# TensorE issues in the order of tracing in four phases of a two-block transformer kernel

## The chip, the cores and the metric

One core of one Trainium2 chip. A core has TensorE (PE, matmuls and transposes, results into PSUM banks), VectorE (DVE), ScalarE (ACT), GpSimd (POOL) and SyncE (SP, which issues the loads). The metric is the device time of one execution in microseconds, and lower is better.

## The reference

Two transformer blocks on one sequence of 512 tokens and 1024 features, in float32. The first block has four mixers (convolution, sparse attention, latent attention, stick breaking) and a feed forward. The second has a gated linear recurrence beside a windowed attention, an attention into 256 memory tokens, and a gated feed forward with a convolution. Cut to the lines that the change touches:

```python
x = x + jnp.square(jax.nn.relu(h2 @ ffn_w1[l])) @ ffn_w2[l]            # first feed forward
...
proj = n @ w_in                                                        # second block's mixers
...
y_rec = o.astype(n.dtype) @ w_br_rec                                   # o: the gated recurrence
qa = partial_rotary(q_a.reshape(B, S, ATT_Q_HEADS, ATT_HEAD_DIM), positions)
ka = partial_rotary(k_a.reshape(B, S, ATT_KV_HEADS, ATT_HEAD_DIM), positions)
y_att = window_gqa_sink(qa, ka, va, sink) @ w_br_att                   # 8 heads, window of 128
merged = jax.nn.sigmoid(gate_r) * y_rec + jax.nn.sigmoid(gate_a) * y_att
return merged @ w_out
...
s = jnp.einsum('bshd,bmhd->bhsm', q, k).astype(jnp.float32) * (MEM_HEAD_DIM ** -0.5)   # memory attention
p = jax.nn.softmax(s, axis=-1).astype(v.dtype)
o = jnp.einsum('bhsm,bmhd->bshd', p, v).reshape(B, S, D_MODEL)
return o @ w_o
...
return (jax.nn.silu(gc) * u) @ w_down                                  # second feed forward
```

## The kernel before, in words

**Data.** The activations stay in SBUF, transposed, as eight tiles x0 to x7 of 128 features by 512 tokens. A matrix product is done in three matmuls, of the high and low parts of both operands (`mm3`, L183 to L185): hi by hi, lo by hi, hi by lo. Weights come from HBM through `wraw`; ACT rounds them to `whi` (L258), and DVE takes the difference as `wlo` (L259). `whi` and `wlo` have two buffers each.

**Phases**, with their place in the profiled execution: the first block's mixers (0 to about 309 us, not touched by the change), the first feed forward `ffn1` (to about 697), the second block's mixers `mixers2` (to about 1047), the memory attention `memory` (to about 1245), the second feed forward `ffn2` (to the end).

**What sets the order.** The program is traced once, call by call. Each instruction then goes to its engine's own list; the framework's scheduler, which models the engines, orders each list, and may let a later traced instruction overtake one that would wait. An engine runs its list strictly in that order, and waits at an instruction whose inputs or whose buffer are not ready. Beside that, the code writes an order by hand: `pipeline` runs the units of an attention in three stages (logits, transposes of the probabilities, product with V), and between the stages calls `fill`, which draws triples of matmuls from a generator `side()` of independent work.

**mixers2.** The recurrence ends with `gla_out`, whose `tr` transposes (L1634) give the operand recT (`rT0` to `rT3`). Then comes the windowed attention. `window` rotates q and k in place (DVE, L1649 to L1652), and then traces its preparation without a `fill` in between:

```python
for c in range(4):
    qT += self.trans_pair(wp, [qkv[:, t, c * P:(c + 1) * P] for t in range(NT)], eighth, f"wq{c}")
...
    kd = self.T(wp, [P, NT, 2, 64], F32, "wkd", 1)
...
    kT.append(self.trans_hl(wp, [kd[:, t].rearrange("p a d -> p (a d)") for t in range(NT)], P, None, f"wk{kh}", ps="pT"))
```

Each `trans_pair` makes four transposes of q into one PSUM bank `pT` (L866), and then `split_pair` reads that bank four times in turn: ACT `wq h` (L880), DVE (L881), ACT `wq l`, DVE. `trans_hl` does the same for k from `wkd`, a copy that POOL makes (L1667), with one read by ACT (`wk h`, L191) and one by DVE (`wk l`, L192). There is one `pT` bank, and one `wkd`. The 32 units of the attention (4 token tiles by 8 heads) follow, with L889 and L890 as their logits, and `self.pipeline(units, 0.6, (0, 2, 3))` draws from `side()`: recT by w_br_rec, and then the gates, columns 4352 on of w_in. Behind the units stands `trans_hl` four times on the attention's result `oN` (16 transposes, L854), in the same `pT` bank.

**memory.** `token_bcast` (L431 on) turns the norm's row sums into a tile by two diagonal matrices in `nsq` (DVE, L437) and a matmul `pt` (L439). The buffers of `nsq` are shared with the squares that POOL adds into `nacc` (L417). A head's probabilities times V are twelve matmuls into a bank `o` (one buffer), which ACT and DVE read out as H2h, H2l, H3h, H3l (L191, L192).

Of the kernel before, what the change touches and what calls it, by code (L numbers as in the profile page):

```python
# [148 lines left out]
class Kern:  # L149
# [382 lines left out]
    def run(self):  # L532
        nc, tc, A = self.nc, self.tc, self.A
        self.setup()
        self.x = [self.T(self.xp, [P, S], F32, f"x{k}") for k in range(8)]
        self.mixers1()
        if self.upto in ("sb", "nsa", "mla", "conv", "x1"):
            return
        self.ffn1()
        if self.upto == "x2":  # L540
            return
        self.mixers2()
        if self.upto in ("gla", "win"):
            return
        self.memory()
        if self.upto in ("x3", "x4"):
            return
        self.ffn2()


    def mixers1(self):
# [1390 lines left out]
```

## Time and profile before

| | |
|---|---|
| time of the kernel before, median of 3 runs | 1624.3 us (1623.17 to 1624.51) |
| profiled execution, its own time | 1626.29 us |
| profiled execution, span from the first to the last instruction | 1624.6 us |
| mean granted clock of TensorE | 0.995 of full |
| TensorE busy | 1591.5 us, 98% |
| TensorE weight loads | 1341.8 us, 83% |
| DVE, ACT, POOL busy | 921.0, 667.0, 174.9 us |

The profiled execution took 2.0 us longer than the median, and 1.7 us more than its span. TensorE is busy nearly throughout: all its idle time together is 1624.6 - 1591.5 = 33.1 us. Matmuls are pipelined, so their durations overlap, and the time that one takes of the engine is read from start to start.

### The profile page before, as it was taken

The page shows a single profiled execution, that of the slowest core. Times are in us where ns is not written, and L with a number is a line of the kernel's source. Part 1 is how long each engine was busy: PE and PEld are TensorE (multiplying, and loading weights), DVE is VectorE, ACT ScalarE, POOL GpSimd, SP SyncE. Part 2 cuts the span into 40 slices and gives each one's busy share as a digit, 9 for nine tenths or more (in the row PEclk, how much of TensorE's full clock was granted, in tenths as well). Part 3 has the DMA queues.
Part 4 walks back from the last instruction along what each step waited for, and adds up shares of the span by engine and source line. Part 5 has one row for each costly group of instructions (what it writes and reads, how often), then busy time and mean ns, then how long its engine had stood idle before and what let it go on. Part 6 is the DMA issues. An engine that isn't in the chain of part 4 may idle for free.

```text
span 1624.6 us, 20813 instructions
## 1 busy us (share of the span) xinstructions
PE 1591.5 (98%) x8049; PEld 1341.8 (83%) x8049; DVE 921.0 (57%) x1503; ACT 667.0 (41%) x1172; POOL 174.9 (11%) x185
## 2 busy tenths in 40 slices
PE   8999999999999999999999999999999999999998
PEld 6798888788888888878888788888988888888886
DVE  6666885644223434475766565664667556526662
ACT  5675554544123423334333354353544233222332
POOL 0121110200000001121110000330002111001110
PEclk9999999999999999999999999999999999999999
DMA  7242131232322223221222211323332333232331
GB/s 225 67 126 85 33 117 40 66 102 92 101 94 98 97 94 100 88 89 55 73 72 78 65 40 59 115 96 118 126 98 84 99 98 97 94 101 91 101 120 52
DMA packets 108118, 148.15 MB, mean 91 GB/s; under 512 B 7887, under 2 KB 58868, under 8 KB 108020
## 3 DMA queue, kind: packets, MB, share of 16 engines
q1 hardware_dynamic: 107876, 146.72, 28.3%
q8 instruction: 63, 1.03, 0.3%
q14 instruction: 35, 0.29, 0.1%
q10 hardware_dynamic: 144, 0.11, 0.0%
HBM read 142.31 MB, written 4.20 MB: 90 GB/s over the span
## 4 chain that ended last, share of the span: by engine, by line
PE 90%; DVE 4%; ACT 2%; issue 1%; POOL 1%; DMA 1%; SPq 0%; POOLq 0%; DVEq 0%; ACTq 0%
PE mm L183 25%; PE mm L185 25%; PE mm L184 25%; PE o L844 2%; PE lv L1570 2%; PE pT L833 1%; PE o L1613 1%; DVE wlo L259 1%; ACT whi L258 1%; PE L L889 1%; DMA wraw<-w_in_dram 1%; DMA wraw<-w_down_dram 1%; PE o L183 0%; PE o L185 0%; PE L L890 0%
## 5 line engine op out<-in xcount | busy, mean ns | idle before, releaser
L259 DVE TENSOR_TENSOR wlo<-wraw,whi 128x1024 fp32r<-128x1024 f32 (+4 forms) x268 | 319.5, 1194 | 439.2 <-ACT whi L258 434.5
L258 ACT ACTIVATE whi<-wraw 128x1024 fp32r<-128x1024 f32 (+4 forms) x268 | 270.4, 1010 | 536.9 <-PE mm L184 470.2
L417 POOL TENSOR_TENSOR nacc<-nacc,nsq 128x512 f32<-128x512 f32 x24 | 37.3, 1553 | 508.7 <-ACT nsq L415 507.6
L1866 POOL TENSOR_TENSOR fz<-fz,fu 128x512 f32<-128x512 f32 x22 | 37.4, 1698 | 269.6 <-ACT fz L1865 269.6
L461 DVE TENSOR_TENSOR x<-mm,x 128x512 f32<-128x512 f32 x72 | 48.9, 687 | 19.1 <-PE mm L185 18.8
L183 PE MATMUL mm<-H4h,whi 128*128 128x512 f32 x147 | 59.3, 404 | 0.0
L183 PE MATMUL mm<-H0h,whi 128*128 128x512 f32 x139 | 55.8, 402 | 2.9 <-ACT whi L258 2.9
L183 PE MATMUL mm<-H6h,whi 128*128 128x512 f32 x147 | 58.1, 399 | 0.4 <-ACT H6h L194 0.4
L183 PE MATMUL mm<-H7h,whi 128*128 128x512 f32 x147 | 58.3, 397 | 0.0
L185 PE MATMUL mm<-H4h,wlo 128*128 128x512 f32 x147 | 57.6, 392 | 0.7 <-DVE wlo L259 0.7
L183 PE MATMUL mm<-H5h,whi 128*128 128x512 f32 x147 | 58.1, 395 | 0.0
L185 PE MATMUL mm<-H6h,wlo 128*128 128x512 f32 x147 | 57.7, 393 | 0.0
L185 PE MATMUL mm<-H5h,wlo 128*128 128x512 f32 x147 | 57.7, 393 | 0.0
L184 PE MATMUL mm<-H6l,whi 128*128 128x512 f32 x147 | 57.7, 393 | 0.0
L184 PE MATMUL mm<-H5l,whi 128*128 128x512 f32 x147 | 57.4, 391 | 0.0
L184 PE MATMUL mm<-H4l,whi 128*128 128x512 f32 x147 | 57.4, 391 | 0.0
L185 PE MATMUL mm<-H7h,wlo 128*128 128x512 f32 x147 | 57.4, 390 | 0.0
L184 PE MATMUL mm<-H7l,whi 128*128 128x512 f32 x147 | 57.3, 390 | 0.0
L185 PE MATMUL mm<-H2h,wlo 128*128 128x512 f32 x139 | 54.5, 392 | 1.1 <-DVE wlo L259 1.1
L183 PE MATMUL mm<-H3h,whi 128*128 128x512 f32 x139 | 55.4, 399 | 0.0
L183 PE MATMUL mm<-H2h,whi 128*128 128x512 f32 x139 | 55.2, 397 | 0.0
L183 PE MATMUL mm<-H1h,whi 128*128 128x512 f32 x139 | 54.9, 395 | 0.0
(1264 smaller groups left out, 4340.1 us busy)
## 6 DMA issues: line engine op xcount, KB each, us to landing
wraw<-ffn_w_dram SPq DMA_DIRECT2D x64, 512.0 KB, 3.6
wraw<-w_up_dram SPq DMA_DIRECT2D x88, 256.0 KB, 2.8
wraw<-w_in_dram SPq DMA_DIRECT2D x36, 512.0 KB, 3.4
wraw<-w_down_dram SPq DMA_DIRECT2D x22, 512.0 KB, 3.6
wraw<-w_mem_kv_dram SPq DMA_DIRECT2D x16, 512.0 KB, 3.7
wraw<-w_in_dram SPq DMA_DIRECT2D x52, 128.0 KB, 2.3
wraw<-w_in_dram SPq DMA_DIRECT2D x20, 256.0 KB, 2.8
wraw<-cmp_w_dram SPq DMA_DIRECT2D x8, 512.0 KB, 4.0
```

The costliest lines, as they stand in the source:

```text
L183: mm(out, a.hi, b.hi, start=start, stop=False, skip_group_check=skip)
L184: mm(out, a.hi, b.lo, start=False, stop=False, skip_group_check=skip)
L185: mm(out, a.lo, b.hi, start=False, stop=stop, skip_group_check=skip)
L258: nc.scalar.activation(hi, raw, AF.Copy)
L259: nc.vector.tensor_sub(lo, raw, hi.bitcast(F32))
L417: eng.tensor_add(nm.acc, nm.acc, sq[:, :nm.N])
L461: self.nc.vector.tensor_add(self.x[k], b, self.x[k])
L833: nc.tensor.transpose(b[:, t * P:(t + 1) * P], st["p"][:, t * P:(t + 1) * P], self.ident)
L844: nc.tensor.matmul(o(), st["pT"][:, t * P:(t + 1) * P], v(t), start=(t == 0), stop=(t == nt - 1))
L889: self.nc.tensor.matmul(out, q[h][:, qs], k.hi[:, ks], start=True, stop=False)
L1570: nc.tensor.matmul(b[:, t * P:(t + 1) * P], ym[:, t * P:(t + 1) * P], mix(X, c, t * P, P), start=True, stop=True)
L1866: nc.gpsimd.tensor_mul(z, z, us[c])
```

## The change

Four phases are traced under a manual schedule for TensorE: there TensorE's list is the order of tracing. The lists of the other engines are still made by the scheduler, which now models a TensorE that doesn't reorder. No instruction is added, taken away or altered.

```diff
--- before
+++ after
@@ -536,16 +536,20 @@
-        self.ffn1()
+        with tc.manual_schedule(engines={mybir.EngineType.PE}):
+            self.ffn1()
...
-        self.mixers2()
+        with tc.manual_schedule(engines={mybir.EngineType.PE}):
+            self.mixers2()
...
-        self.memory()
+        with tc.manual_schedule(engines={mybir.EngineType.PE}):
+            self.memory()
...
-        self.ffn2()
+        with tc.manual_schedule(engines={mybir.EngineType.PE}):
+            self.ffn2()
```

In all, 509 of TensorE's 7547 instructions change their place in its list (none in ffn2), 70 of ACT's 1025 and 121 of DVE's 1503; none of POOL's or SP's. Lines of the changed kernel from L541 on are four higher than the same lines before (L854 is L858, L866 is L870, L889 is L893, L1634 is L1638). Numbers behind a name count tiles as they are made and run 5 to 8 higher after the change; "x4" stands for four such rows.

**First place: TensorE, the preparation of the window attention in mixers2.** Before, from the last transposes `tr` of the recurrence on (recT by w_br_rec into `mm_7857`, `mm_7858`, and q's transposes into the bank `pT_7774`):

```order
L1634 MATMUL tr_7715<-cmat_78,go_7676 128x128 x4
L183 MATMUL mm_7857<-rT0h_6626,whi_7862 128x512
L184 MATMUL mm_7857<-rT0l_6627,whi_7862 128x512
L185 MATMUL mm_7857<-rT0h_6626,wlo_7863 128x512
L183 MATMUL mm_7857<-rT1h_7061,whi_7862 128x512
L184 MATMUL mm_7857<-rT1l_7062,whi_7862 128x512
L185 MATMUL mm_7857<-rT1h_7061,wlo_7863 128x512
L183 MATMUL mm_7858<-rT0h_6626,whi_7862 128x512
L184 MATMUL mm_7858<-rT0l_6627,whi_7862 128x512
L185 MATMUL mm_7858<-rT0h_6626,wlo_7863 128x512
L183 MATMUL mm_7858<-rT1h_7061,whi_7862 128x512
L866 MATMUL pT_7774<-cmat_78,qkv_5936 128x128
```

In the changed kernel, from the same transposes on:

```order
L1638 MATMUL tr_7720<-cmat_78,go_7681 128x128 x4
L870 MATMUL pT_7779<-cmat_78,qkv_5941 128x128 x4
L870 MATMUL pT_7790<-cmat_78,qkv_5941 128x128 x4
L870 MATMUL pT_7801<-cmat_78,qkv_5941 128x128 x4
L870 MATMUL pT_7812<-cmat_78,qkv_5941 128x128 x4
L858 MATMUL pT_7826<-cmat_78,wkd_7823 128x128 x4
L858 MATMUL pT_7838<-cmat_78,wkd_7835 128x128 x4
L893 MATMUL L_7848<-wk0h_7831,wq0h_7784 128x256
L894 MATMUL L_7848<-wk0l_7832,wq0h_7784 128x256
L893 MATMUL L_7856<-wk0h_7831,wq0l_7787 128x256
L894 MATMUL L_7856<-wk0l_7832,wq0l_7787 128x256
L183 MATMUL mm_7862<-rT0h_6631,whi_7867 128x512
```

All 24 transposes and the first four logits now stand directly behind `tr`. The 106 matmuls that stood between them before (recT by w_br_rec, and the first of the gates) come behind, in triples between the stages of the attention's units.

**Second place: TensorE, the transposes of the attention's result `oN` in mixers2.** Before (`mm_8601` and `mm_8602` are gates):

```order
L854 MATMUL pT_8624<-cmat_78,oN_7842 128x128 x4
L183 MATMUL mm_8601<-H1h_5475,whi_8565 128x512
L184 MATMUL mm_8601<-H1l_5476,whi_8565 128x512
L185 MATMUL mm_8601<-H1h_5475,wlo_8566 128x512
L183 MATMUL mm_8602<-H0h_5463,whi_8565 128x512
L184 MATMUL mm_8602<-H0l_5464,whi_8565 128x512
L185 MATMUL mm_8602<-H0h_5463,wlo_8566 128x512
L183 MATMUL mm_8602<-H1h_5475,whi_8565 128x512
L854 MATMUL pT_8633<-cmat_78,oN_7842 128x128 x4
L184 MATMUL mm_8602<-H1l_5476,whi_8565 128x512
```

and likewise for the third and fourth group. In the changed kernel:

```order
L858 MATMUL pT_8629<-cmat_78,oN_7847 128x128 x4
L858 MATMUL pT_8638<-cmat_78,oN_7847 128x128 x4
L858 MATMUL pT_8647<-cmat_78,oN_7847 128x128 x4
L858 MATMUL pT_8656<-cmat_78,oN_7847 128x128 x4
L183 MATMUL mm_8606<-H1h_5477,whi_8570 128x512
L184 MATMUL mm_8606<-H1l_5478,whi_8570 128x512
L185 MATMUL mm_8606<-H1h_5477,wlo_8571 128x512
```

The four groups of transposes stand in a row; the 21 matmuls that stood between them (seven each time) come behind.

**Third place: TensorE, the norm's matmul `pt` in memory.** Before, it stands behind the rest of the matmuls `mm_9172` and `mm_9173` of the mixers' output and five matmuls of the memory's keys (`mm_9370`):

```order
L184 MATMUL mm_9173<-H7l_8944,whi_9265 128x512
L185 MATMUL mm_9173<-H7h_8943,wlo_9266 128x512
L183 MATMUL mm_9370<-mH0h_9035,whi_9302 128x256
L184 MATMUL mm_9370<-mH0l_9036,whi_9302 128x256
L185 MATMUL mm_9370<-mH0h_9035,wlo_9303 128x256
L183 MATMUL mm_9370<-mH1h_9061,whi_9302 128x256
L184 MATMUL mm_9370<-mH1l_9062,whi_9302 128x256
L439 MATMUL pt_9338<-nsq_9335,ones_79 128x256
L185 MATMUL mm_9370<-mH1h_9061,wlo_9303 128x256
```

In the changed kernel (`mm_9179` and `mm_9180` are `mm_9171` and `mm_9172` of before):

```order
L183 MATMUL mm_9179<-H7h_8948,whi_9273 128x512
L184 MATMUL mm_9179<-H7l_8949,whi_9273 128x512
L185 MATMUL mm_9179<-H7h_8948,wlo_9274 128x512
L439 MATMUL pt_9346<-nsq_9343,ones_79 128x256
L183 MATMUL mm_9180<-H6h_8936,whi_9273 128x512
L184 MATMUL mm_9180<-H6l_8937,whi_9273 128x512
```

It moved 17 instructions forward: twelve of the mixers' output and five of the keys now stand behind it.

## Rows read from the trace of the kernel before

**Rows 1.** The page: busy time, share of the span and instructions of each engine.

```profile
PE 1591.5 (98%) x8049; PEld 1341.8 (83%) x8049; DVE 921.0 (57%) x1503; ACT 667.0 (41%) x1172; POOL 174.9 (11%) x185
```

**Rows 2.** Busy time by stretch; columns: length, PE, PEld, DVE, ACT, POOL, clock, DMA.

```profile
697.00:913.00 216.00, 211.23 (x1172) 183.21 (x1171) 145.41 (x224) 83.25 (x136) 27.97 (x20) 0.99 0.23 71
913.00:942.00 29.00, 28.69 (x136) 22.31 (x137) 22.50 (x42) 12.35 (x18) 3.31 (x7) 1.00 0.25 78
942.00:1001.00 59.00, 58.88 (x400) 52.68 (x399) 36.48 (x105) 34.69 (x95) 0.00 (x0) 1.00 0.11 35
...
1245.00:1600.00 355.00, 354.60 (x1572) 292.98 (x1571) 197.42 (x232) 104.10 (x124) 44.82 (x27) 1.00 0.30 95
```

**Rows 3.** Timeline, PE at 911: start, duration, engine, line, operation.

```profile
911.24 0.39 PE L184 MATMUL mm<-H7l,whi 128*128 128x512 f32 x1
911.47 0.39 PE L185 MATMUL mm<-H7h,wlo 128*128 128x512 f32 x1
```

**Rows 4.** Timeline of the window's preparation, from PE, ACT, DVE and POOL.

```profile
918.49 0.32 DVE L1652 TENSOR_TENSOR qkv<-qkv,wu 128x160 f32<-128x160 f32 x1
...
929.53 0.63 PE L866 MATMUL pT<-cmat,qkv 128*128 128x128 f32 x4
...
930.20 0.69 ACT L880 ACTIVATE wq2h<-pT,w 64x512 fp32r<-64x512 f32 x1 [2.14 <-PE pT L866]
...
930.92 0.74 DVE L881 SCALAR_TENSOR_TENSOR wq2h<-pT,w,wq2h 64x512 fp32r<-64x512 f32 x1 [1.53 <-ACT wq2h L880]
...
931.69 0.68 ACT L880 ACTIVATE wq2l<-pT,w 64x512 fp32r<-64x512 f32 x1 [0.81 <-DVE wq2h L881]
...
932.41 0.76 DVE L881 SCALAR_TENSOR_TENSOR wq2l<-pT,w,wq2l 64x512 fp32r<-64x512 f32 x1 [0.75 <-ACT wq2l L880]
...
933.31 0.63 PE L866 MATMUL pT<-cmat,qkv 128*128 128x128 f32 x4
...
939.25 0.60 ACT L191 ACTIVATE wk0h<-pT 128x512 fp32r<-128x512 f32 x1 [0.29 <-PE pT L854]
...
939.35 1.48 POOL L1667 COPY wkd<-qkv 128x256 f32<-128x256 f32 x2 [19.73 <-PE pT L854]
...
940.13 0.68 DVE L192 TENSOR_TENSOR wk0l<-pT,wk0h 128x512 fp32r<-128x512 f32 x1
```

**Rows 5.** Timeline, transposes of `oN` at 1005 (PEld is the weight load).

```profile
1005.62 0.61 PE L854 MATMUL pT<-cmat,oN 128*128 128x128 f32 x4
...
1007.65 0.42 PEld L854 LDWEIGHTS pT<-cmat,oN 128*128 128x128 f32 x4 [0.22 <-DVE rT2l L192]
1007.71 0.60 PE L854 MATMUL pT<-cmat,oN 128*128 128x128 f32 x4
```

**Rows 6.** Timeline around `pt` in memory, from PE, POOL and DVE.

```profile
1086.83 0.39 PE L183 MATMUL mm<-H6h,whi 128*128 128x512 f32 x1
...
1088.41 3.02 POOL L417 TENSOR_TENSOR nacc<-nacc,nsq 128x512 f32<-128x512 f32 x2 [6.05 <-ACT nsq L415]
...
1090.22 1.49 DVE L437 TENSOR_SCALAR nsq<-cmat,rs 128x128 f32<-128x128 f32 x2
...
1091.86 0.67 PE L439 MATMUL pt<-nsq,ones 128*128 128x256 f32 x2 [1.56 <-DVE nsq L437]
```

**Rows 7.** Timeline between two products with V in memory.

```profile
1193.81 0.28 PE L183 MATMUL L<-K4h,Q4h 128*128 128x256 f32 x1
...
1194.24 1.23 DVE L259 TENSOR_TENSOR wlo<-wraw,whi 128x1024 fp32r<-128x1024 f32 x1 [0.20 <-ACT whi L258]
...
1196.86 0.31 PE L183 MATMUL o<-mpTh,Vh 128*128 128x256 f32 x1
```

**Rows 8.** TensorE's clock: a wait, the window behind it, the same line slow and fast.

```profile
706.52 1.67 PE L1555 MATMUL lv<-gq,gym 128*128 128x128 f32 x8 [2.23 <-POOL gym L1549]
707.98 1.91 PE L1570 MATMUL lv<-gX,gym 128*128 128x128 f32 x8
...
834.51 1.13 PE L1570 MATMUL lv<-gX,gym 128*128 128x128 f32 x8
...
707.00:711.00 4.00, 4.00 (x20) 3.78 (x19) 2.63 (x4) 1.17 (x2) 0.00 (x0) 0.57 0.40 131
```

## The prediction

> **What bounds the kernel now.** I read the page first: TensorE is busy 98% of the span, the next engine 57% [rows 1]. So the end is set by TensorE's work plus the time in which it stands still, and a change that only reorders TensorE can only alter the second term. I then read the busy time by stretch, to see where TensorE stands still in the four phases that the change touches. It is little: 4.77 us between 697 and 913, 0.31 in the preparation of the window attention, 0.12 in the attention's units, 0.40 from 1245 to 1600 [rows 2], and 1.56 ahead of `pt` in memory [rows 6]; together 7.2 us. That is the most that a better order could take away. Third, the timeline at each place where the lists of before and after differ, to see what the instruction that moved forward waits for. A 128x512 matmul starts 0.23 us behind the one before it [rows 3]; with that pitch I count the work that used to cover a wait.
>
> **The change part by part.** No instruction is added, and ffn2's list is the same, so all work and all transfers stay as they are; SP's and POOL's lists don't change at all. Each moved piece costs the cover that it loses, and this can't be earned back later, because TensorE has almost no idle time behind it to fill.
>
> *Preparation of the window attention.* This is the large term. Before, from 913.0 to 942.0 TensorE did 24 transposes, four logits and 106 matmuls of other work, and stood still for 0.31 us [rows 2]. Now the transposes follow each other with nothing between. The first group waits for the rotation of q, which ends on DVE at 918.49 + 0.32 = 918.8 [rows 4]. Each group then needs the single `pT` bank, which is free again only when ACT, DVE, ACT and DVE have read it in turn: 0.69, 0.74, 0.68 and 0.76 us. The groups that started at 929.53 and 933.31 show this chain undisturbed: 3.78 us from one to the next [rows 4]. So the q groups start at 918.8, 922.6, 926.4 and 930.2, and the first k group at 933.9. The second k group needs `wkd` refilled: 0.67 us for the transposes (ACT starts that long behind them, 929.53 to 930.20), then 1.48 us on POOL, which is longer than 0.60 on ACT and 0.68 on DVE [rows 4]. It starts at 936.1; with 0.67 for it and about 0.5 for the logits, TensorE gets to the units at 937.3 instead of 942.0, that is 4.7 us earlier, but with 106 x 0.23 = 24.4 us of work not done. Net cost: **19.7 us**. Bounds: 18 if ACT and DVE, freed of the other work's evacuations, shorten the cycle to the bare 2.87 + 0.63 = 3.5 us; 21.5 if the copies or the rotation come 1.8 us later. That work now lies between the units' stages, which have 59 us of it already.
>
> *Transposes of `oN`.* Before, each group started 2.09 us behind the last (1005.62, 1007.71). The weight loads of four transposes take 0.42, and 0.22 was idle already [rows 5], so 2.09 - 0.42 - 0.22 = 1.45 us of other work was in between. Three such gaps open: **4.4 us**. Bounds: 3.0 (a bank read out in 1.0) to 4.8 (all 21 matmuls at 0.23).
>
> *`pt` in memory.* It is issued 17 instructions earlier, at 1086.83 instead of behind 1.56 us of idle at 1091.86. The matmuls that it overtakes ran from 1086.83 to 1090.1 = 3.3 us. It needs the diagonals that DVE makes from 1090.22, in buffers that POOL's two additions from 1088.41 (1.5 us each) give free [rows 6]. Nothing in TensorE's order makes these earlier, so the wait grows to about 5 us, net **3.3 us**. Bounds: 1.5 (one POOL addition less ahead of it) to 4.1.
>
> *Product with V.* The second head's twelve matmuls into `o` move ahead of the logits and seven projections that ran from 1193.81 to 1196.86. The one `o` bank comes free only then, behind two reads each by ACT and DVE with a 1.23 us weight split between them [rows 7]. Net **3.0 us**, bounds 1.8 (the split out of the way) to 3.1.
>
> *Four small places.* At the start of ffn1 two matmuls are followed directly by the one that needs `wlo`, which takes DVE 1.23 us [rows 7] and was covered by ten other instructions: 0.8 (0 to 1.2). Three matmuls moved behind the wait for `gym` at 704: 3 x 0.23 = 0.7 (0 to 0.7). Two half-size ones at 834: 0.2 (0 to 0.3). Three behind a product with V at 1229: 0.6 (0 to 0.7). Together **2.3 us**.
>
> *Clock.* Behind the 2.23 us wait at 704 the granted clock was 0.57 over 4 us, close to the lower level of 1.2 GHz; this cost 4 x 0.43 = 1.7 us [rows 8]. Behind the 1.56 us wait ahead of `pt` I see no such fall. The new waits of about 3 us or more are three: the window's preparation, `pt`, the product with V. Three times 1.7 is 5.1. Inside the preparation the transposes would run slowly too: eight matmuls of this size took 1.91 instead of 1.13 us [rows 8], so four take 0.39 longer, and six groups 2.3. Together **7.4 us**, bounds 1.7 (one fall) to 9 (the gaps at `oN` count too).
>
> The Trainium skill ("TensorE: Matmul & The Clock Gate", section "Why this matters for your kernels") asks only that longer gaps than this 2.23 us be kept out; the trace disagrees, since here the clock fell behind it. By that section only the two longest waits would cost clock, and the sum would be about 1.7 us lower.
>
> **Sum.** 19.7 + 4.4 + 3.3 + 3.0 + 2.3 + 7.4 = 40.1 us. On the profiled execution's own 1626.3 us that is 1666.4. Its time was 2.0 above the median of the runs, so I forecast **1664.4 us**, 2.5% slower. With all low bounds together the sum is 26.0 us (1650), with all high ones 45.7 (1670).
>
> **The rivals.**
>
> *Faster.* The scheduler's list is made from a model; where that model is wrong it left 7.2 us of idle, of which 2.23 at 704 also cost 1.7 us of clock. If tracing order removed all of it, the time would be 1624.3 - 8.9 = 1615. For this the preparation would have to cost less than 8.9 us: 24.4 - (942.0 - end) < 8.9 means that it ends before 926.5, 7.7 us behind the rotation; with five steps between six groups that is a cycle of at most 1.5 us. The four reads of one bank alone take 2.87 [rows 4]. And the lists show these waits untouched or made longer. Chance 0.02.
>
> *No change.* The order could be the same in effect, since most of TensorE's list is. Against it stand the rows of the lists: six transposes' groups directly behind each other in one bank. Chance 0.03.
>
> *Partly regained.* If busy TensorE hides slack, the 24.4 us of moved work could fit between the units at less than its price. Weight loads fill 52.7 of the 59 us there [rows 2]; if the other 6.3 were free, the time would be 1658. Against it: in the preparation 106 matmuls at 0.23 leave only 4.6 of 29 us for 24 transposes and four logits, so nothing is hidden there. Chance 0.08. The Trainium skill ("Perfetto Trace Analysis", section "Identifying the Most-Contended Engine") says that matmul busy time is no good measure of headroom and that the share of weight loads is; that is this rival's rule. The start to start pitch in this trace speaks against it.
>
> *No clock lost*, or one fall only: 1664.4 - 5.7 = 1659. Chance 0.07.
>
> *The units wait too.* In the new list the 32 units carry 207 other matmuls instead of 105. If DVE or ACT, which now also read out the moved work there, came 0.4 us late in each, this would add 13 us: 1677. DVE was busy 36.5 and ACT 34.7 of 59 us [rows 2]; with five more weight splits of 1.23 and eight evacuations like the 0.68 one of [rows 4] DVE comes to 48 of 83. That is slack, so the chance is 0.07.
>
> **How the numbers follow.** The sum as it stands (within its bounds) has 0.73, the rivals the rest. The time is that of the sum, 1664.4. The range 1645 to 1680 takes in the bounds of the sum, "partly regained", "no clock lost" and the lower half of "the units wait too"; outside remain the first two rivals, the other half and what I overlooked, below 2 in 10. About 0.2% (3 us) is what a measurement of this kernel can tell from no change. Slower by more has 0.95 (all but the first two), within it 0.03, faster 0.02.
>
> **What would show it right or wrong.** In the changed profile TensorE should stand still for about 20 us between 913 and 937, in five or six waits for DVE of some 3 us, each ahead of transposes; the transposes of `oN` should show three waits of 1.3 to 1.6 us; `pt` one of about 5 us on DVE; the product with V one of about 3 us. TensorE's idle time should grow from 33 to some 66 us, and its granted clock should fall behind the three long waits. The stretch of the units should grow from 59 to about 83 us with hardly any idle. I am wrong if the preparation is over before 930, if the units' stretch grows by clearly less than the moved 24 us, or if idle time outside these places shrinks by more than 5 us.

## The result, and the profile after

The changed kernel takes 1668.8 us (median of 4 runs, 1666.28 to 1670.44) against 1624.4 us before: ratio 1.0274, 95% interval 1.0256 to 1.0292. The forecast was 1664.4 us, with a range from 1645 to 1680. The profiled execution took 1666.28 us, with a span of 1664.6 us, 40.0 us longer than the span before. The forecast for a profiled execution was 1666.4; the median lies 2.5 us above this one, where I had taken 2.0 us off.

The page's first line, busy time by engine, answers to [rows 1]:

```profile
PE 1600.8 (96%) x8049; PEld 1348.8 (81%) x8049; DVE 921.7 (55%) x1503; ACT 668.5 (40%) x1172; POOL 172.3 (10%) x185
```

The instructions are the same. TensorE's idle time went from 33.1 to 1664.6 - 1600.8 = 63.8 us, and its busy time rose by 9.3 us with no instruction added. About 7.5 us of that is time at the lower clock: in the three slow stretches shown below, busy time times the missing share of the clock is 8.54 x 0.48 + 3.51 x 0.42 + 3.84 x 0.50. The rest is probably the ends of matmuls. In [rows 3] a 128x512 matmul lasts 0.39 us and the next starts 0.23 us behind it, so each new wait behind one uncovers some 0.16 us that overlapped before (an estimate). The other engines do the same work in a longer span.

The waits of TensorE, longest first; columns: what waited for what, us in total, times, longest:

```profile
PE pt L439 <- DVE nsq L437: 5.2, 1, 5.2
...
PE pT L858 <- DVE wq3l L885: 3.3, 1, 3.3
PE pT L870 <- DVE wq0l L885: 3.2, 1, 3.2
PE pT L870 <- DVE wq1l L885: 3.1, 1, 3.1
PE pT L870 <- DVE wq2l L885: 3.1, 1, 3.1
...
PE lv L1559 <- POOL gym L1553: 2.9, 1, 2.9
PE o L183 <- DVE H3l L192: 2.8, 1, 2.8
PE pT L870 <- DVE qkv L1656: 2.3, 3, 1.2
PE pT L870 <- DVE rT3l L195: 2.2, 1, 2.2
PE pT L858 <- DVE wk0l L192: 1.5, 1, 1.5
...
PE pT L858 <- DVE rT0l L192: 1.4, 1, 1.4
PE pT L858 <- DVE rT2l L192: 1.4, 1, 1.4
PE pT L858 <- DVE rT1l L192: 1.4, 1, 1.4
```

Of the list before, only two of these were there, `lv` with 2.2 us and `pt` with 1.6 [rows 6, 8]. Each of the others stands where the order is new: transposes into `pT` directly behind each other, and a product with V directly behind another one. The one name that looks odd is `rT3l` ahead of the first transpose: it is the last reading of the recurrence's bank `tr`, and the code gives the banks of one phase back before it takes those of the next.

The window preparation in the timeline of TensorE (start, duration, line, operation, idle before and its releaser):

```profile
919.82 0.48 PE L870 MATMUL pT<-cmat,qkv 128*128 128x128 f32 x1 [1.18 <-DVE qkv L1656]
923.52 1.08 PE L870 MATMUL pT<-cmat,qkv 128*128 128x128 f32 x4 [3.23 <-DVE wq0l L885]
927.76 1.08 PE L870 MATMUL pT<-cmat,qkv 128*128 128x128 f32 x4 [3.15 <-DVE wq1l L885]
931.99 1.09 PE L870 MATMUL pT<-cmat,qkv 128*128 128x128 f32 x4 [3.15 <-DVE wq2l L885]
936.34 1.09 PE L858 MATMUL pT<-cmat,wkd 128*128 128x128 f32 x4 [3.26 <-DVE wq3l L885]
938.93 1.08 PE L858 MATMUL pT<-cmat,wkd 128*128 128x128 f32 x4 [1.50 <-DVE wk0l L192]
939.66 0.56 PE L893 MATMUL L<-wk0h,wq0h 128*128 128x256 f32 x1
```

Read it against [rows 4]: a group now follows the last by 4.24 us where it was 3.78. The reads by ACT and DVE last as long as before; the four transposes take 1.08 instead of 0.63 us, and these 0.45 us are the difference. TensorE reaches the first logits at 939.66, where the forecast had 936.8 without the clock and 939.1 with it; of that, 0.96 us came in ahead of the preparation (the table below).

Busy time by stretch, for the preparation, the units behind it, and what follows the waits at `oN` and at `pt` (columns as in [rows 2]; the third from the right is the granted clock, 0.5 of full being 1.2 GHz):

```profile
920.00:943.00 23.00, 8.54 (x33) 6.31 (x33) 8.68 (x16) 8.97 (x15) 1.30 (x4) 0.52 0.07 23
943.00:1026.00 83.00, 82.94 (x505) 72.46 (x503) 44.89 (x110) 37.38 (x95) 0.00 (x0) 1.00 0.15 46
1031.00:1035.00 4.00, 3.51 (x12) 2.99 (x13) 1.12 (x2) 0.60 (x1) 0.00 (x0) 0.58 0.00 0
1122.00:1126.00 4.00, 3.84 (x9) 3.11 (x10) 0.06 (x2) 0.38 (x1) 0.00 (x0) 0.50 0.00 0
```

The stretch of the units is 83 us long, as forecast (59 + 24.4), with 0.06 us of idle: the work taken out of the preparation cost its full price there. DVE, at 45 of 83 us, had slack.

Where the 40 us came in can be read from the start of the same instruction in both traces. The first block's mixers, which have the same lists, ended 0.8 us earlier this time.

| instruction | before | after | later by | so the step cost |
|---|---|---|---|---|
| last two `tr` of the recurrence | 912.66 | 913.62 | 0.96 | three small places, with the 0.8: 1.8 |
| first transposes of `oN` | 1001.49 | 1025.34 | 23.85 | window preparation 22.9 |
| `pt` of the memory's row sums, L426 | 1080.88 | 1110.90 | 30.02 | transposes of `oN` 6.2 |
| first transposes of the memory's probabilities | 1165.94 | 1202.48 | 36.54 | `pt` of the norm 6.5 |
| fifth such transposes | 1202.27 | 1241.82 | 39.55 | product with V 3.0 |
| first transposes of the output | 1592.29 | 1632.28 | 39.99 | the rest 0.4 |

### The profile page after: what moved, and what is told of

It reads as the page before. It is cut to its first block, busy times and chain, and to the rows that moved or that the text cites. A ratio compares the mean times of both kernels' runs of the same rounds, so it can differ in the third digit from the quotient of the medians.

```text
span 1664.6 us, 20814 instructions
## 1 busy us (share of the span) xinstructions
PE 1600.8 (96%) x8049; PEld 1348.8 (81%) x8049; DVE 921.7 (55%) x1503; ACT 668.5 (40%) x1172; POOL 172.3 (10%) x185
## 4 chain that ended last, share of the span: by engine, by line
PE 88%; DVE 5%; ACT 3%; issue 1%; POOL 1%; DMA 1%; SPq 0%; POOLq 0%; ACTq 0%; DVEq 0%
PE mm L183 25%; PE mm L185 25%; PE mm L184 24%; PE o L848 2%; PE lv L1574 2%; DVE wlo L259 1%; PE pT L837 1%; PE o L1617 1%; ACT whi L258 1%; PE L L893 0%; PE o L183 0%; PE L L894 0%; PE o L950 0%; PE o L185 0%; PE o L184 0%
## 5 line engine op out<-in xcount | busy, mean ns | idle before, releaser
L259 DVE TENSOR_TENSOR wlo<-wraw,whi 128x1024 fp32r<-128x1024 f32 (+4 forms) x268 | 319.5, 1194 | 441.4 <-ACT whi L258 433.4
L1870 POOL TENSOR_TENSOR fz<-fz,fu 128x512 f32<-128x512 f32 x22 | 37.4, 1701 | 269.3 <-ACT fz L1869 269.3
```

The lines of the kernel that those rows point to most:

```text
L259: nc.vector.tensor_sub(lo, raw, hi.bitcast(F32))
L1870: nc.gpsimd.tensor_mul(z, z, us[c])
```

## The experiments

Each kernel ran in turns with the kernel before on the same chip; differences are to the median of before there (1625.7 to 1626.0 us).

**One phase alone, three kernels.** The manual schedule stays around one part and is taken off the others:

```diff
-        with tc.manual_schedule(engines={mybir.EngineType.PE}):
-            self.ffn1()
+        self.ffn1()
```

> TensorE in tracing order in the second block's mixers alone; the scheduler orders the two feed forwards and the memory attention. My theory: the loss is a sum of separate waits, and this phase holds the window preparation (22.9 us in the trace of the change, clock included), the transposes of the attention's result (6.2) and two small places (about 1), so the time is 1624.4 + 30 = 1654, from 1651 to 1658. Rival, the phases interact (lists of the other engines, made anew, shift work into the later phases): the parts alone don't add up, and this one is under 1648 or over 1661.

Measured: 1656.9 us, ratio 1.0189 (1.0175 to 1.0203), +31.1.

> TensorE in tracing order in the memory attention alone. My theory: pt of the norm (6.6 us in the trace of the change, clock included), the product with V (3.0, without a fall of the clock, up to 5 with one) and a small place (0.7), so 1624.4 + 10 = 1634.7, from 1633 to 1638. Rival, the phases interact: the wait for pt was late because the mixers ran late, and alone the phase costs under 5 us.

Measured: 1637.1 us, ratio 1.0067 (1.0053 to 1.0081), +11.3. The wait of `pt` is the same 5.16 us as in the change, so it is not late because the mixers ran late.

> TensorE in tracing order in the two feed forwards alone. My theory: only the start of the first feed forward has another list, worth 0.8 us (0 to 1.2): 1625.2, no difference that this measurement can tell. Rival, tracing order is better in a phase of plain products, because nothing there depends on a model: faster by 3 us or more.

Measured: 1627.1 us, ratio 1.0006 (0.9997 to 1.0015), +1.3: no difference that can be told.

The three add to 43.7 us; the change costs 44.4. The loss is a sum of separate places.

**The preparation covered again, tracing order kept.** `side()` is queued ahead of the preparation, which draws from it:

```diff
-                oN, units = self.window(wp, qkv)
...
+                oN, units = self.window(wp, qkv, (7, 5, 5, 5, 5, 3))
...
         for c in range(4):
+            self.fill(gaps[c])                 # 7, 5, 5, 5
             qT += self.trans_pair(...)
...
+            self.fill(gaps[4 + kh])            # 5, 3
             kT.append(self.trans_hl(...))
...
-                self.pipeline(units, 0.6, (0, 2, 3))
+                self.pipeline(units, 0.3, (0, 2, 3))
```

> TensorE in tracing order in all four phases as in the change, but the tracing now lays 33 triples of the independent matmuls between the groups of the window preparation, and fewer between the attention's units. My theory: the preparation's 22.9 us come back, since its chain runs beside 7, 5, 5, 5, 5 and 3 triples of 0.69 us, as long as the scheduler's order had there: 1668.8 - 22.9 = 1646, from 1643 to 1650. Rival, in-order issue costs by itself (each wait on another engine now holds all that stands behind it, and moving work away from the units opens waits there instead): 1655 or more.

Measured: 1651.2 us, ratio 1.0153 (1.0137 to 1.0168), +25.4 instead of the change's +44.4: 19.0 of the 22.9 us came back. In time that is 1.2 us above the expected range; as a difference to the kernel before, which took 1.4 us more on this chip, it is at the range's upper end (+25.6) and under the rival's +30.6. (The gaps hold 30 triples, 7 + 4 x 5 + 3; the 33 above is a slip.) What is missing stands in its timeline as smaller waits, at the preparation and at the first units:

```profile
922.08 0.33 PE L870 MATMUL pT<-cmat,qkv 128*128 128x128 f32 x1 [0.47 <-DVE qkv L1656]
926.35 0.63 PE L870 MATMUL pT<-cmat,qkv 128*128 128x128 f32 x4 [0.51 <-DVE wq0l L885]
...
939.53 0.63 PE L858 MATMUL pT<-cmat,wkd 128*128 128x128 f32 x4 [1.18 <-DVE wq3l L885]
...
945.29 0.44 PE L837 MATMUL pT<-cmat,wp 128*128 128x128 f32 x2 [1.16 <-ACT wp L832]
```

**Two banks in the preparation.** The groups alternate between `pT` and the logits' banks:

```diff
-            qT += self.trans_pair(wp, [...], eighth, f"wq{c}")
+            qT += self.trans_pair(wp, [...], eighth, f"wq{c}", ps=("pT", "L")[c % 2])
```

and the same for the two k groups.

> The change, with the six groups of the window preparation alternating between the bank pT and the two logits banks, which are idle then. My theory: the 4.24 us from group to group come from the one bank, which ACT, DVE, ACT and DVE read in turn; with a second bank the next group's transposes and first read run beside, and a group costs about 2.3 us (ACT's two reads and the handing over between ACT and DVE). Five steps shorter by 1.9: about 9 us less than the change's +44.4 over the kernel before, so +35, from +32 to +39. Rival, the transposes themselves (1.1 us each at the low clock), the rotation or POOL's copies set the pace: +42 or more.

Measured: 1664.2 us, ratio 1.0235 (1.0220 to 1.0250), +38.1, which is 6.3 less than the change. In the timeline of TensorE two groups now take the time of one:

```profile
920.70 1.06 PE L870 MATMUL L<-cmat,qkv 128*128 128x128 f32 x4
924.20 1.08 PE L870 MATMUL pT<-cmat,qkv 128*128 128x128 f32 x4 [2.43 <-DVE wq0l L885]
925.07 1.06 PE L870 MATMUL L<-cmat,qkv 128*128 128x128 f32 x4
928.68 1.09 PE L858 MATMUL pT<-cmat,wkd 128*128 128x128 f32 x4 [2.54 <-DVE wq2l L885]
```

A pair of groups follows the last pair by 4.48 us, where one group took 4.24, so a group costs 2.24 (expected: about 2.3). The bank set the pace. From `tr` to the first logits it is 17.2 us instead of 26.0, a gain of 8.8; 2.5 of it were lost on the way to the end. The profile shows 0.7 us of wait behind the first logits, and a product with V that cost 2.7 us more than in the change (42.0 instead of 39.3 us from the first to the fifth transposes of the probabilities): here the clock fell behind it, at 0.50 from 1227 to 1232, and in the profile of the change it did not.

**The clock held up by work of no use.**

```diff
+        def busy(n):
+            b = self.ps("mm")
+            for i in range(n):
+                self.mm3(b, recT[0][:, :P], recT[1], start=i == 0, stop=i == n - 1)
         for c in range(4):
+            busy(6 if c == 0 else 3)
             qT += self.trans_pair(...)
...
+            busy(3 - 2 * kh)
             kT.append(self.trans_hl(...))
```

> The change, with 66 matmuls of no use put into the waits of the window preparation (18 ahead of the first group, 9 ahead of each of the next four, 3 ahead of the last; their sums go into banks that nothing reads, the output stays the reference's). They fit into the waits at full clock (9 x 0.23 = 2.1 of 3.1 us). My theory: 3.6 of the change's cost are the clock (0.45 us for each of six groups, and 1.1 on the first logits and matmuls behind them); with TensorE kept busy the granted clock stays 1.00 there, a group costs 3.8 instead of 4.24 us, and the time is 3.6 us lower, +41 over the kernel before, in spite of 15 us more work. Rival, the clock doesn't matter there, or the added work comes on top: +44 to +60.

Measured: 1668.4 us, ratio 1.0258 (1.0242 to 1.0273), +42.4, which is 2.0 less than the change. These intervals overlap, so the time alone doesn't decide; the timeline does. (18 + 4 x 9 + 3 is 57 matmuls, as many as the page counts more; the 66 above is a slip. They leave nothing of the kernel out.)

```profile
924.63 0.63 PE L870 MATMUL pT<-cmat,qkv 128*128 128x128 f32 x4 [1.17 <-DVE wq0l L885]
928.42 0.63 PE L870 MATMUL pT<-cmat,qkv 128*128 128x128 f32 x4 [1.07 <-DVE wq1l L885]
932.20 0.63 PE L870 MATMUL pT<-cmat,qkv 128*128 128x128 f32 x4 [1.08 <-DVE wq2l L885]
```

A group takes 0.63 us again, and 3.79 from one to the next. From `tr` (914.86) to the first logits (938.61) it is 23.75 us instead of 26.04: the clock cost 2.3 us up to there, as the forecast had it, and matmuls of no use in a wait cost nothing. Of the 1.1 us that I expected behind the logits nothing came back, since ACT's first exponentials, behind a table load of 1.28 us, became what TensorE waits for there (1.16 us).

**`pt` later, and the last product with V covered.**

```diff
-                yield
-                yield
+                for _ in range(5):
+                    yield
                 mn.R = self.token_bcast(mn.rs, 256, "pt")
...
-            self.drain()
...
-                for _ in g:
-                    pass
+                for i, _ in enumerate(g):
+                    if i == 8:
+                        self.drain()
...
-            self.pipeline([... for h in (0, 1) for qh in range(2)], (5, 5, 5), (0, 1, 2))
+            self.pipeline([... for h in (0, 1) for qh in range(2)], (4, 4, 4), (0, 1, 2))
```

`drain` finishes the queued work, `pt` among it; it now comes behind eight steps of the next projection instead of ahead of it.

> The change, with pt of the memory's norm traced about 33 matmuls later and the last gap between two products with V filled with twelve matmuls (the gaps before it get four triples instead of five). My theory: pt's 6.6 us and the product's 2.8 come back, 9.4 in all: +35 over the kernel before, from +32 to +38. Rival, the diagonals and the reading of the bank come later too, as other work of DVE and POOL moves ahead of them: +40 or more.

Measured: 1663.1 us, ratio 1.0230 (1.0213 to 1.0247), +37.1, which is 7.3 less than the change. The wait at the product with V is gone. Half of `pt`'s wait is still there, and the rival was right for that half (timeline of POOL, DVE and TensorE):

```profile
1118.97 4.74 POOL L417 TENSOR_TENSOR nacc<-nacc,nsq 128x512 f32<-128x512 f32 x3 [6.05 <-ACT nsq L415]
...
1127.12 0.47 DVE L437 TENSOR_SCALAR nsq<-cmat,rs 128x128 f32<-128x128 f32 x2
1127.73 1.19 PE L439 MATMUL pt<-nsq,ones 128*128 128x256 f32 x2 [2.50 <-DVE nsq L437]
```

Traced later, the diagonals get a later turn in the shared buffers `nsq`. They now stand behind three additions on POOL and one on DVE, and came at 1127.12. In the change they stood behind two additions on POOL, and the first of them came at 1119.77, held by one of these:

```profile
1119.77 1.39 DVE L437 TENSOR_SCALAR nsq<-cmat,rs 128x128 f32<-128x128 f32 x1 [1.16 <-POOL nacc L417]
```

**A buffer of their own for the diagonals**, in the change and in the kernel before.

```diff
-        dg = self.T(self.sp, [P, NT, P], F32, "nsq", 2)[:, :nt]
+        dg = self.T(own, [P, 2, P], F32, "dg", 1) if own else self.T(self.sp, [P, NT, P], F32, "nsq", 2)[:, :nt]
...
-                mn.R = self.token_bcast(mn.rs, 256, "pt")
+                mn.R = self.token_bcast(mn.rs, 256, "pt", kp)
```

> The change, with the two diagonal matrices ahead of pt in a buffer of their own instead of one shared with the squares that POOL adds up. My theory: pt's wait of 5.2 us is the wait for that buffer; with its own, the diagonals are made as soon as the row sums are there, long before TensorE comes to pt, and the wait goes with its fall of the clock: 6.6 less, +38 over the kernel before, from +35 to +40. Rival, pt waits for the row sums' chain or for DVE's other work: +43 or more.

Measured: 1663.1 us, ratio 1.0228 (1.0214 to 1.0242), +37.4, which is 7.0 less than the change. The diagonals are made behind POOL's reciprocal roots, 4.4 us ahead of `pt`, which doesn't wait at all:

```profile
1112.30 0.70 POOL L226 TENSOR_TENSOR rs<-rst,mhalf 128x2 f32<-128x2 f32 x1 [4.40 <-DVE rst L209]
1113.04 0.48 DVE L437 TENSOR_SCALAR dg<-cmat,rs 128x128 f32<-128x128 f32 x2 [0.82 <-POOL rs L226]
...
1117.47 0.59 PE L439 MATMUL pt<-dg,ones 128*128 128x256 f32 x2
```

So the whole wait was for the buffer.

> The kernel before, with the same buffer of its own for the diagonals. My theory: its 1.56 us of idle ahead of pt goes, -1.6, from -3 to 0. Rival, the scheduler lays the list anew and puts another wait there: 0 or slower.

Measured: 1625.5 us, ratio 0.9999 (0.9990 to 1.0008). The wait of 1.56 us is gone there too, but the time is the same. As the rival had it, there is another wait instead: behind `pt` TensorE now waits 1.00 us for a `wlo` (L259) that DVE makes late. The rest is less than this measurement tells.

**Everything covered by hand, and once more.** Both kernels fill each place that lost its cover; the first has 9, 6, 5, 5, 7 and 3 triples in the preparation and a rate of 0.3 in the units, the second a rate of 0.22:

```diff
-                    if h == 0:
-                        self.fill(5)
+                    if h == 0:
+                        self.fill(9)
...
+                    if c:
+                        self.fill(3)
                     attT.append(self.trans_hl(...))
```

(the second has 7 instead of 9, leaves memory to the scheduler, and gives the diagonals their own buffer).

> Tracing order in the second block's mixers and the memory attention, the feed forwards left to the scheduler, and every place that lost its cover given one by hand in the tracing: 9, 6, 5, 5, 7 and 3 triples in the window preparation, three more behind the first logits, three between the transposes of the attention's result, 12 instead of 8 yields ahead of pt's wait, four instead of five triples in each gap of the memory's first two heads (so that some are left for the last gap), and four triples more ahead of the recurrence's first wait for POOL (2.9 us in the change). My theory: all the loss is lost cover, none is tracing order as such, so the time is that of the kernel before, +0, from -5 to +5, and below it if the wait for POOL is covered too (-3). Rival, issue in a fixed order costs a remainder everywhere, which no filling gives back: +8 or more.

Measured: 1641.8 us, ratio 1.0098 (1.0083 to 1.0113), +15.8. That is the rival's time. But TensorE's 12.3 us of added idle (45.4 instead of 33.1; its busy time rose by another 5.0) are not spread everywhere; most of it stands in a few new waits. At the recurrence's first wait TensorE now loses 0.21 instead of 2.9 us, and at its end, where that work is missing, 2.5. `pt` waits 2.5 as above. And in the units it waits 5.5 us in all for ACT, 0.9 for `wp` and 4.6 for `wpT`. The row in its list of waits, and ACT's timeline, which shows why:

```profile
PE pT L834 <- ACT wpT L838: 4.6, 4, 1.6
```

```profile
998.90 1.28 ACT L1508 ACT_TABLE_LOAD   x1
1000.19 0.63 ACT L1508 ACTIVATE v<-v 128x512 f32<-128x512 f32 x1
1000.84 1.28 ACT L829 ACT_TABLE_LOAD   x1
```

With more triples spent early, the first half of the gates was done before the units were. The scheduler, which still orders ACT, then put its sigmoids between the exponentials, each with two table loads of 1.28 us (13 loads in all instead of 7).

> Tracing order in the second block's mixers alone, the other phases left to the scheduler; the mixers' waits filled by hand as in the run with everything filled, but with fewer triples between the attention's units (so that the first half of the gates isn't done before the units are, and its sigmoids, which cost ACT two table loads of 1.28 us each time, don't come between the exponentials), and two more triples instead of four at the recurrence's first wait. The memory's diagonals get a buffer of their own. My theory: the rest of +15.8 over the kernel before was made of new waits of that filling (5 us in the units, 2.5 at the recurrence's end, 4 with their clock in memory), so +0 to +4 here, and 1.6 of that comes back by the diagonals' own buffer: +1, from -2 to +4. Rival, a fixed order costs a remainder everywhere: +8 or more.

Measured: 1630.8 us, ratio 1.0028 (1.0017 to 1.0040), +5.1 by the medians. This lies between the two ranges. Of the change's 44.4 us, 39.3 are back, but not all by filling: memory and the feed forwards are left to the scheduler here. The fair measure is the mixers alone, where filling took +31.1 down to +5.1. No version in tracing order beats the kernel before. The table loads are 7 again. What is left of waits that the kernel before doesn't have are pieces of 0.4 to 1.1 us: 0.83 and 0.91 within the recurrence (for ACT) and 1.13 at its end, 0.84 and 0.64 in the preparation, 0.50 and 0.77 and smaller ones in the units. The recurrence's first wait, 1.55, is shorter than the 2.23 of before. Whether better filling would remove the rest is not shown.

## Why the prediction was right

**Idle is all that order can change.** Right, with the clock as the term of its own that the prediction made of it: the span rose by TensorE's new idle, 30.7 us, and by 9.3 us of busy time, about 7.5 of them clock.

**Preparation, 19.7 without and 23.7 with the clock.** Measured 22.9. The chain through one bank is shown by the run with two banks, the clock's 2.3 us by the run with work of no use, and that no part is earned back by the 83 us of the units' stretch.

**Transposes of `oN`, 4.4.** Measured 6.2. The three waits are 1.41 us each, as forecast, but two things were mis-sized. One is the lost cover. I took 0.22 us off each gap as idle already, but in [rows 5] that idle stands at the weight load (PEld), and the matmul row of TensorE shows none. The four groups lie 6.15 us apart, from the first to the last, where they lay 6.22 (1001.49 to 1007.71):

```profile
1025.34 0.60 PE L858 MATMUL pT<-cmat,oN 128*128 128x128 f32 x4
...
1031.49 1.11 PE L858 MATMUL pT<-cmat,oN 128*128 128x128 f32 x4 [1.41 <-DVE rT2l L192]
```

So the 21 matmuls between them, at 0.23 us each, were lost nearly whole: 4.8 us, my upper bound. The other is the clock, which makes the remaining 1.4. I had kept it only as an upper bound, since 1.4 us is less than the 1.56 us behind which I saw no fall. Three such gaps with only four transposes between them let it fall (0.58 at 1031, above).

**`pt`, 3.3 and 1.7 for the clock.** Measured 6.5. The mechanism is shown by the diagonals' own buffer. The wait is 5.16 us against about 5 forecast, 3.6 more than before. The clock cost 3.84 x 0.50 = 1.9 rather than 1.7; the trace has a further wait of 0.58 us for a `wlo` at 1131, which I didn't foresee.

**Product with V, 3.0 and 1.7 for the clock.** Measured 3.0; the wait of 2.76 us is as forecast, and the clock did not fall behind it in this profile. It did in the five other profiles with this wait (below). So this term was too large here by 1.7, which hides that the two above were too small.

**Small places, 2.3.** Measured 1.8 up to the recurrence's end, and 0.4 behind: 2.2.

**The sum.** That 40.1 meets 40.0 is in part luck. The transposes of `oN` and `pt` came out 3.3 us above their terms with the clock, the preparation and the product with V 2.5 below theirs, and the first block, which the change doesn't touch, ended 0.8 earlier. (The upper bounds of the prediction add to 45.4 us, not 45.7; nothing hangs on it.)

**The rivals.** "Partly regained" (1658) fell with the units' stretch: moved work cost its full price. The rule of the Trainium skill that was weighed there ("Perfetto Trace Analysis", "Identifying the Most-Contended Engine") did not guide here: weight loads were busy 52.7 of the 59 us of that stretch before [rows 2], and the other 6.3 us took up none of the moved work. "No clock lost" fell too. The Trainium skill's advice to keep out long gaps ("TensorE: Matmul & The Clock Gate", "Why this matters for your kernels") does not cover what cost clock at `oN`: three gaps of 1.41 us were enough there. "The units wait too" did not happen in the change, but did in the run with everything covered, by a way that I hadn't thought of: the order that the scheduler gives to ACT.

**The size.** The median is 4.4 us above the forecast. 2.0 of that is the deduction for how the profiled execution of before stood to its median, which doesn't carry over: here the profiled one was the fastest of four. The other 2.4 comes with the spread of the changed kernel's runs, 4.2 us against 1.4 before. That the clock's falls make this spread is likely: they come or don't come at the same waits, and the mean granted clock was 0.985 in the profiled run and 0.983 in the three slower ones. The kernel before shows the same in its 39 runs beside the experiments: 1624.8 us on average where that clock was 0.997 (11 runs), 1626.3 where it was 0.995 (19 runs). Which fall the profiled run lacked is not shown; the one behind the product with V would fit.

## What to carry to other kernels

Where one engine is busy 98% of the time, look for what its order covers: for each instruction that moves forward, read from the trace when its inputs and its buffer are free, and price the wait with the work that used to stand there; here each term so priced came within 1.8 us of the measured one. Code that traces a chain through a single bank or buffer without a fill between its steps relies on a scheduler to cover it, and has to say so by hand before the order of tracing is frozen. Covering by hand is a budget: work spent at one wait is missing at the next, and what gets done early on one engine may be ordered badly on another that the scheduler still controls.

## What the runs showed of the hardware

**The clock's fall behind a wait of 2 to 3 us is not certain.** The same wait, in kernels with the same instructions around it, was followed by a fall in some profiles and not in others. The first row is the kernel before behind its 2.23 us wait for `gym`; the second the run with memory alone, with the same list and the same 2.23 us (columns as in [rows 2]):

```profile
706.00:711.00 5.00, 4.48 (x21) 4.25 (x22) 3.63 (x5) 1.17 (x2) 0.47 (x1) 0.66 0.32 105
```

```profile
707.00:712.00 5.00, 4.65 (x27) 4.24 (x28) 4.54 (x6) 1.29 (x2) 0.29 (x1) 1.00 0.38 105
```

Behind the 2.76 us wait at the product with V, the change (first) kept its clock and the run with memory alone (second) did not:

```profile
1233.00:1238.00 5.00, 4.73 (x32) 4.43 (x33) 1.67 (x4) 1.41 (x5) 0.00 (x0) 1.00 0.32 105
```

```profile
1203.00:1208.00 5.00, 4.23 (x23) 4.24 (x24) 1.27 (x3) 1.02 (x3) 0.00 (x0) 0.66 0.31 105
```

Over all profiles, the wait of 2.23 us was followed by a fall in three of four, and that of 2.76 in five of six. The wait of 5.16 us at `pt` was followed by a slow `pt` (1.19 us for its two matmuls, against 0.67 in [rows 6]) in all five profiles that have it. So a single profile gives such a term with an error of its whole size, 1.7 us.

**Short waits add up.** Three waits of 1.41 us with four transposes between were followed by a fall in each of the seven profiles that have them, by the third or the fourth group. The single wait of 1.56 us at `pt` was followed by none in the three profiles that have it. The kernel before could have warned me: in its first block, waits of 0.39 and 1.43 us at 218 and 221 were followed by a granted clock of 0.50 from 223 to 225.
